# Dilated attention mix of a two-layer encoder: group weights turned once on TensorE and spread over the channels by DMAs from a DRAM scratch row, in place of copies and transposes

## The chip, the core and the metric

The kernel runs on one core of a Trainium2 chip. The metric is the device time of one execution in microseconds (us); lower is better.

## The reference, cut to what matters

A residual trunk of two layers (`DEPTH = 2`), 1024 tokens of 1024 channels, everything in float32. In each layer h = RMSNorm(x) goes through one input projection; its parts feed four mixers (Fourier, convolution, attention, pooling), each gated, projected by `w_branch[n]` and weighted by a sigmoid merge gate; the sum goes through `w_out`. The attention mixer runs three dilated window attentions of four heads each and mixes them by the softmax of their log-sum-exps, one weight for each token, head and group:

```
def dilated_mixture(qkv, cos, sin):
    ...
    for g, (window, dil) in enumerate(DILATED_CFG):            # 3 groups
        o, l = dilated_window_attention(q[:, :, g], k[:, :, g], v[:, :, g], dil, window // (2 * dil))
        ...
    alpha = jax.nn.softmax(jnp.stack(lses, axis=0), axis=0)
    out = outs[0] * alpha[0][..., None].astype(outs[0].dtype)
    for g in range(1, N_ATT_GROUPS):
        out = out + outs[g] * alpha[g][..., None].astype(outs[g].dtype)
```

The kernel computes the same weights from each group's maximum m and denominator d: alpha_g = exp(m_g - max m) / sum over the groups of d exp(m - max m), with the outputs of a group not yet divided.

## The kernel before

Activations lie channels by tokens: a tile is 128 channels x 512 tokens, tokens in two halves `hf`. Matrix products run with operands split in a high and a low part (three matmuls a product). The four heads are two head pairs `hp` (two heads x 64 channels = 128 partitions), so `att_mix` (L556) runs once for each head pair in each layer, four times in all. Names in this text: the **mix** is one run of `att_mix`; the first mix of a layer belongs to hp 0, the second to hp 1.

Order of the work. `layer` (L1135) writes one long stream of products; `att_group` and `att_mix` are generators in lanes. After every second pair of a main product, `passes` (L123) calls `tick`, which moves each lane one step, up to its next `yield`; `self.wait(n)` yields n times. So a mix's instructions are strewn between the matmuls that stand there. The first mix of a layer falls among the products of the second head pair's q, k, v; the second at the end of the input projection (tile z) and the start of the branch projections (tile py, `branch` L930, weights wr loaded at L116, split by ACT at L105 and DVE at L106). Each engine runs its own list in order, SP issues nearly all DMAs, and an instruction that waits holds up all behind it on its engine.

One mix before: maxima and sums on tiles of 128 tokens x 16 (8 token tiles x 2 heads), three exps of 128x16 on ACT (L572), weights es[g]. Then for each half and each group, six times: DVE copies a group's weights over the 64 channels of a head (tile fx, 128 tokens x 512, L588); SP loads the group's outputs, channels by tokens, from DRAM (tile og, L590); four PE transposes turn fx into a PSUM bank (tile fb, L594, one of the five `aux` banks); DVE multiplies og by fb (L595) and adds up (L597). The sum goes to DRAM (att, L600), one DMA for each half.

What stands around the second mix: `gate_evac` (L603) computes gates (ACT sg, L609; DVE gp, L610). `branch` runs over the four branches in the order pool, Fourier, attention, convolution. The inputs of a branch are made by `gated` (L906): for each of four quarter tiles, a load from a parked DRAM tensor (tile unpark, L926; `park` for pooling, `four`, `att`, `conv`), then a split into g, the high part on ACT (L105), the low part on DVE (L106). Branch outputs y leave PSUM by ACT (L938) and go to DRAM by SP (L939). fx, og, unpark, y, sg and others share one pool of twelve 128x512 tiles (`t2`, L94).

Of the kernel before, what the change touches and what calls it, by code (L numbers as in the profile page):

```python
# [9 lines left out]
F32 = mybir.dt.float32  # L10
F32R = mybir.dt.float32r
AF = mybir.ActivationFunctionType
ALU = mybir.AluOpType

P = 128
# [31 lines left out]
class Net:  # L47
# [505 lines left out]
        nc.sync.dma_start(out=nat, in_=sc.rearrange("(t p) c -> p t c", p=P))  # L553
        done.append((od, nat))

    def att_mix(self, groups, park):  # L556

        nc = self.nc
        while len(groups) < 3:
            yield  # L560
        yield from self.wait(4)
        sm = lambda nm: self.sm.tile([P, 8, 2], F32, tag="x" + nm, name="x" + nm, bufs=2)
        ms = [st[:, :, 0:2] for _, st in groups]
        ds = [st[:, :, 2:4] for _, st in groups]
        m = sm("m")
        nc.vector.tensor_tensor(out=m, in0=ms[0], in1=ms[1], op=ALU.max)
        nc.vector.tensor_tensor(out=m, in0=m, in1=ms[2], op=ALU.max)
        es = []
        for g in range(3):
            e = sm(f"e{g}")  # L570
            nc.vector.tensor_tensor(out=e, in0=ms[g], in1=m, op=ALU.subtract)
            nc.scalar.activation(out=e, in_=e, func=AF.Exp)  # L572
            es.append(e)
        z, t = sm("z"), sm("t")
        nc.vector.tensor_tensor(out=z, in0=ds[0], in1=es[0], op=ALU.mult)
        for g in (1, 2):
            nc.vector.tensor_tensor(out=t, in0=ds[g], in1=es[g], op=ALU.mult)
            nc.vector.tensor_tensor(out=z, in0=z, in1=t, op=ALU.add)
        nc.vector.reciprocal(out=z, in_=z)
        for g in range(3):  # L580
            nc.vector.tensor_tensor(out=es[g], in0=es[g], in1=z, op=ALU.mult)
        yield from self.wait(2)
        for hf in range(2):
            sl = slice(hf * H, hf * H + H)
            out = None
            for g in range(3):
                f = self.t2("fx").rearrange("p (t h c) -> p t h c", t=4, h=2)
                nc.vector.tensor_copy(out=f, in_=es[g][:, 4 * hf:4 * hf + 4].unsqueeze(3).to_broadcast([P, 4, 2, 64]))  # L588
                og = self.t2("og")
                nc.sync.dma_start(out=og, in_=groups[g][0][:, sl])  # L590
                yield from self.wait(4)
                ps = self.aux("fb")
                for j in range(4):
                    nc.tensor.transpose(ps[:, j * P:(j + 1) * P], f[:, j].rearrange("p h c -> p (h c)"), self.ident)  # L594
                nc.vector.tensor_tensor(out=og, in0=og, in1=ps, op=ALU.mult)  # L595
                if g:
                    nc.vector.tensor_tensor(out=out, in0=out, in1=og, op=ALU.add)  # L597
                else:
                    out = og
            nc.sync.dma_start(out=park[:, sl], in_=out)  # L600
# [534 lines left out]
    def layer(self, l):  # L1135
        nc = self.nc
        pool = self.pool(l)
        att = self.dr.tile([2, P, S], F32, name=f"att{l}")
        for hp in range(2):
            done = []  # L1140
            for g in range(3):
                self.att_group(l, hp, g, done)
            self.start("mix", self.att_mix(done, att[hp]))
        uf = [self.fourier_in(l, c) for c in range(2)]
        res, fy = [], []
        self.start("fou", self.fourier_pq(l, uf, res))
        self.start("fou", self.fourier_out(l, res, fy))
        conv = self.dr.tile([2, P, S], F32, name=f"conv{l}")
        gps = {0: [], 1: [], 2: []}
        four = self.dr.tile([2, P, S], F32, name=f"four{l}")  # L1150
        self.start("fou", self.gate_later(fy, gps[0], four))
        for hf in range(2):
            self.start("taps", self.conv_mix(l, hf, gps[1], conv))
        tf = {i: [] for i in range(1, 5)}
        g = {n: [] for n in range(4)}
        make = {0: self.gated(self.unpark(four), None, g[0]), 1: self.gated(self.unpark(conv), None, g[1]),
                2: self.gated(self.unpark(att), gps[2], g[2]), 3: self.gated(self.unpark(pool), None, g[3])}
        lanes = {0: ("fou",), 2: ("att", "mix"), 1: ("taps",), 3: ()}
        for n in GORDER:
            for c in range(2):  # L1160
                if (n, c) == (GORDER[2], 1):
                    self.start("g", make[YORDER[0]])
                gps[n].append(self.gate_path(l, n, c))
        for i, n in enumerate(YORDER):
            self.finish("g")
            if i < 3:
                for lane in lanes[YORDER[i + 1]]:
                    self.finish(lane)
                self.start("g", make[YORDER[i + 1]])
            if i == FORMS:  # L1170
                self.start("forms", self.token_forms(tf))
            self.branch(l, n, g[n])
        self.finish("forms")
        self.out_proj(l, self.gates(l, tf))
# [97 lines left out]
```

## Time and profile before

| | us |
|---|---|
| median of 3 runs | 1987.56 |
| lowest, highest | 1986.22, 1989.28 |
| profiled execution | 1990.16 |
| its span | 1988.4 |
| PE busy | 1948.0 (98%) |
| DVE busy | 1485.0 (75%) |
| ACT busy | 999.9 (50%) |
| DMA queue q1, share of 16 engines | 37.0% |

The span is the profiled part of the execution; 1.8 us lie outside it. PE is TensorE's matmuls, ACT is ScalarE, DVE is VectorE, SP the engine that issues DMAs. Times in rows are us from the span's start. The granted TensorE clock was 0.998 of full speed. Durations of successive matmuls overlap: what one costs on PE is the step from its start to the next start.

### The profile page before, as it was taken

To read this page: it belongs to the slowest core of one execution; us is meant where nothing else is said; L and a number is where in the kernel's file an instruction comes from. 1 tells how busy PE (TensorE), PEld (TensorE's weight loads), DVE (VectorE), ACT (ScalarE), POOL (GpSimd) and SP (SyncE) were. 2 spreads that over 40 slices of the span, in tenths; PEclk is the share of its full clock that TensorE was granted. 3 is DMA by queue.
4 is the path that set the end of the run, shared out by engine and by line. 5 is a ranking of instruction groups with operands and counts; after the bars stand their busy time and mean duration, and the time that the engine had idled before them with its cause. 6 is when DMAs were issued, how large, how long until landed. Compare 5 with 4: busy or idle time off the path is not lost.

```text
span 1988.4 us, 26782 instructions
## 1 busy us (share of the span) xinstructions
PE 1948.0 (98%) x9484; PEld 1624.7 (82%) x9484; DVE 1485.0 (75%) x2740; ACT 999.9 (50%) x1917; POOL 41.1 (2%) x90
## 2 busy tenths in 40 slices
PE   8999999999999999999999999999999999999997
PEld 6788887888888888887888888888888888888887
DVE  7598878886577777776655888888564877787764
ACT  6336655568574344444431456656775644443441
POOL 0000000000000000000000000000000000000000
PEclk9999999999999999999999999999999999999999
DMA  6243344423774433427421534433248823424443
GB/s 237 78 149 117 102 131 120 128 67 107 247 276 167 156 106 108 157 76 259 163 81 45 159 117 126 133 106 106 87 139 295 287 85 127 136 99 146 170 148 107
DMA packets 129446, 281.08 MB, mean 141 GB/s; under 512 B 32928, under 2 KB 37920, under 8 KB 129312
## 3 DMA queue, kind: packets, MB, share of 16 engines
q1 hardware_dynamic: 118368, 239.52, 37.0%
q0 software_dynamic: 10944, 39.85, 6.0%
q8 instruction: 75, 1.23, 0.3%
q14 instruction: 59, 0.48, 0.1%
HBM read 186.84 MB, written 67.30 MB: 128 GB/s over the span
## 4 chain that ended last, share of the span: by engine, by line
PE 81%; DVE 9%; ACT 4%; DMA 4%; issue 2%; SPq 0%; DVEq 0%; ACTq 0%
PE z L129 24%; PE ga L129 13%; PE g L129 9%; PE gb L129 8%; PE op L129 8%; PE py L129 8%; PE z L256 3%; DVE cv L849 2%; PE pv L129 2%; PE s L466 2%; PE pt L492 1%; DVE w L106 1%; ACT w L105 1%; ACT o L523 1%; DMA mt<-m 1%
## 5 line engine op out<-in xcount | busy, mean ns | idle before, releaser
L129 PE MATMUL z<-h,w 128*128 128x512 f32 x3000 | 741.4, 396 | 2.5 <-DVE gp L610 1.4
L129 PEld LDWEIGHTS z<-h,w 128*128 128x128 f32 x3000 | 546.8, 188 | 109.1 <-DVE gp L610 1.8
L106 DVE TENSOR_TENSOR w<-wr,w 128x1024 fp32r<-128x1024 f32 (+1 forms) x135 | 158.7, 1178 | 106.8 <-ACT w L105 90.9
L105 ACT ACTIVATE w<-wr 128x1024 fp32r<-128x1024 f32 (+1 forms) x135 | 137.9, 1023 | 172.7 <-PE z L129 80.3
L129 PE MATMUL g<-h,wf 128*128 128x512 f32 x768 | 184.5, 389 | 0.0
L129 PE MATMUL ga<-t,wf 128*128 128x512 f32 x768 | 184.5, 389 | 0.0
L129 PE MATMUL gb<-t,wf 128*128 128x512 f32 x768 | 184.5, 389 | 0.0
L129 PE MATMUL op<-m,w 128*128 128x512 f32 (+1 forms) x960 | 179.8, 348 | 2.8 <-DVE m L106 2.7
L849 DVE SCALAR_TENSOR_TENSOR cv<-cv,params 128x512 f32<-128x512 f32 x240 | 179.1, 746 | 2.3
L129 PE MATMUL py<-g,w 128*128 128x512 f32 x768 | 178.4, 391 | 0.8 <-DVE gp L610 0.5
L129 PEld LDWEIGHTS op<-m,w 128*128 128x128 f32 x960 | 153.9, 189 | 27.1 <-DVE m L106 4.4
L129 PEld LDWEIGHTS py<-g,w 128*128 128x128 f32 x768 | 143.1, 188 | 31.7 <-ACT y L938 1.3
L129 PEld LDWEIGHTS ga<-t,wf 128*128 128x128 f32 x768 | 144.2, 188 | 29.9
L129 PEld LDWEIGHTS gb<-t,wf 128*128 128x128 f32 x768 | 144.2, 188 | 29.9
L129 PEld LDWEIGHTS g<-h,wf 128*128 128x128 f32 x768 | 144.2, 188 | 29.9
L105 ACT ACTIVATE wf<-wr 128x512 fp32r<-128x512 f32 x144 | 91.0, 632 | 117.6 <-issue 46.3
L106 DVE TENSOR_TENSOR wf<-wr,wf 128x512 fp32r<-128x512 f32 x144 | 98.8, 686 | 19.4 <-ACT wf L105 18.1
L480 ACT ACTIVATE p<-p,nm 128x256 f32<-128x256 f32 (+2 forms) x192 | 87.9, 459 | 42.7 <-DVE nm L477 42.4
L105 ACT ACTIVATE wf<-s 128x512 fp32r<-128x512 f32 x64 | 40.5, 632 | 105.2 <-PE gb L129 62.6
L129 PE MATMUL ga<-h,wf 128*128 128x512 f32 x384 | 92.2, 389 | 0.0
L523 ACT ACTIVATE o<-pv 64x128 f32<-64x128 f32 x192 | 67.5, 351 | 48.1 <-PE pv L129 46.2
L129 PEld LDWEIGHTS ga<-h,wf 128*128 128x128 f32 x384 | 72.1, 188 | 15.0
(244 smaller groups left out, 2683.0 us busy)
## 6 DMA issues: line engine op xcount, KB each, us to landing
wr<-in_w_in_dram SPq DMA_DIRECT2D x75, 512.0 KB, 3.8
y<-y SPq DMA_DIRECT2D x128, 256.0 KB, 4.1
y<-y POOLq DMA_DIRECT2D x64, 512.0 KB, 4.8
wr<-in_w_gate_dram SPq DMA_DIRECT2D x48, 512.0 KB, 4.4
wr<-in_w_out_dram SPq DMA_DIRECT2D x32, 512.0 KB, 3.6
rot<-rt SPq DMA_DIRECT2D x192, 64.0 KB, 2.0
cv<-in_w_gate_dram SPq DMA_DIRECT2D x16, 512.0 KB, 4.9
wr<-in_w_branch_dram SPq DMA_DIRECT2D x16, 512.0 KB, 4.7
```

The source lines that it names most:

```text
L105: self.nc.scalar.activation(out=hi, in_=src, func=AF.Copy)
L106: self.nc.vector.tensor_tensor(out=lo, in0=src, in1=hi.bitcast(F32), op=ALU.subtract)
L129: self.nc.tensor.matmul(ps, w, x, start=(first and i + u == 0), stop=(i == n - 1 and u == 2), skip_group_check=open_)
L256: self.nc.tensor.matmul(ps, a[:, k], b, start=(k + j == 0), stop=(k == KC - 1 and j == 2))
L466: mm(s[i][h], q[h + j][:, qs], k[h][:, a:a + n], start=(j == 0), stop=(j == 2))
L480: nc.scalar.activation(out=ph, in_=ph, func=AF.Exp, bias=nm[:, h:h + 1], accum_out=st[:, t, 2 + h:3 + h])
L492: nc.tensor.transpose(pt[:rows[ci], cs], p[:, off:off + rows[ci]], self.ident)
L523: nc.scalar.activation(out=dst, in_=src, func=AF.Copy)
L849: self.tc.keep_in_program_order(nc.vector.scalar_tensor_tensor(out=y, in0=u[:, j:j + H], scalar=tap(j), in1=y, op0=ALU.mult, op1=ALU.add))
```

## The change

The three weight tiles are slices of one tile (xe, 128 x 48), so that one exp does for all groups. One PE transpose of 128 x 48 (tile et, an `aux` bank) puts (group, token tile, head) on 48 partitions and tokens in the free dimension; ACT copies it to SBUF (er), SP writes it to a DRAM tensor ed (24 KB). For each half and group two DMAs fill fx with channels on partitions: each reads four rows of 128 tokens of ed and writes them into 64 partitions (a source dimension of stride 0; 128 KB written in pieces of 512 bytes). DVE multiplies og by fx from SBUF. The copies (L588) and the fb transposes (L594) are gone, and the wait between og's load and its use is 3 steps instead of 4. `name` makes the DRAM tensor's name. All later line numbers grow by four.

```diff
@@ -553,7 +553,7 @@
         nc.sync.dma_start(out=nat, in_=sc.rearrange("(t p) c -> p t c", p=P))
         done.append((od, nat))
 
-    def att_mix(self, groups, park):
+    def att_mix(self, groups, park, name):
 
         nc = self.nc
         while len(groups) < 3:
@@ -565,12 +565,11 @@
         m = sm("m")
         nc.vector.tensor_tensor(out=m, in0=ms[0], in1=ms[1], op=ALU.max)
         nc.vector.tensor_tensor(out=m, in0=m, in1=ms[2], op=ALU.max)
-        es = []
+        ea = self.sm.tile([P, 3, 8, 2], F32, tag="xe", name="xe", bufs=2)
+        es = [ea[:, g] for g in range(3)]
         for g in range(3):
-            e = sm(f"e{g}")
-            nc.vector.tensor_tensor(out=e, in0=ms[g], in1=m, op=ALU.subtract)
-            nc.scalar.activation(out=e, in_=e, func=AF.Exp)
-            es.append(e)
+            nc.vector.tensor_tensor(out=es[g], in0=ms[g], in1=m, op=ALU.subtract)
+        nc.scalar.activation(out=ea, in_=ea, func=AF.Exp)
         z, t = sm("z"), sm("t")
         nc.vector.tensor_tensor(out=z, in0=ds[0], in1=es[0], op=ALU.mult)
         for g in (1, 2):
@@ -580,19 +579,24 @@
         for g in range(3):
             nc.vector.tensor_tensor(out=es[g], in0=es[g], in1=z, op=ALU.mult)
         yield from self.wait(2)
+
+        ps = self.aux("et")
+        nc.tensor.transpose(ps[:48, 0:P], ea.rearrange("p g t h -> p (g t h)"), self.ident)
+        er = self.t2("er")
+        nc.scalar.activation(out=er[:48, 0:P], in_=ps[:48, 0:P], func=AF.Copy)
+        ed = self.dr.tile([3, 8, 2, P], F32, name=f"ed_{name}")
+        nc.sync.dma_start(out=ed.rearrange("g t h p -> (g t h) p"), in_=er[:48, 0:P])
         for hf in range(2):
             sl = slice(hf * H, hf * H + H)
             out = None
             for g in range(3):
-                f = self.t2("fx").rearrange("p (t h c) -> p t h c", t=4, h=2)
-                nc.vector.tensor_copy(out=f, in_=es[g][:, 4 * hf:4 * hf + 4].unsqueeze(3).to_broadcast([P, 4, 2, 64]))
-                og = self.t2("og")
+                f, og = self.t2("fx"), self.t2("og")
+                for h in range(2):
+                    nc.sync.dma_start(out=f[64 * h:64 * h + 64].rearrange("p (t n) -> p t n", n=P),
+                                      in_=ed[g, 4 * hf:4 * hf + 4, h].unsqueeze(0).to_broadcast([64, 4, P]))
                 nc.sync.dma_start(out=og, in_=groups[g][0][:, sl])
-                yield from self.wait(4)
-                ps = self.aux("fb")
-                for j in range(4):
-                    nc.tensor.transpose(ps[:, j * P:(j + 1) * P], f[:, j].rearrange("p h c -> p (h c)"), self.ident)
-                nc.vector.tensor_tensor(out=og, in0=og, in1=ps, op=ALU.mult)
+                yield from self.wait(3)
+                nc.vector.tensor_tensor(out=og, in0=og, in1=f, op=ALU.mult)
                 if g:
                     nc.vector.tensor_tensor(out=out, in0=out, in1=og, op=ALU.add)
                 else:
@@ -1140,7 +1144,7 @@
             done = []
             for g in range(3):
                 self.att_group(l, hp, g, done)
-            self.start("mix", self.att_mix(done, att[hp]))
+            self.start("mix", self.att_mix(done, att[hp], f"{l}_{hp}"))
         uf = [self.fourier_in(l, c) for c in range(2)]
         res, fy = [], []
         self.start("fou", self.fourier_pq(l, uf, res))
```

Counts over the four mixes, from the loops: 24 DVE copies, 96 fb transposes in 24 groups of four, and 8 of 12 exps go; 4 et transposes, 4 er copies, 4 DMAs to ed and 48 DMAs ed to fx come (48 x 128 KB = 6.3 MB).

How the engines' lists change at three places. First SP's list in the first layer where the second mix begins, at the end of the input projection, before the change (`wr` of `w_branch` are branch weights, `park` is the parked pooling, `od` a group's outputs):

```order
L116 DMA wr<-in_w_branch_dram 128x1024
L590 DMA og<-od_1_0_3598 128x512
L926 DMA unpark<-park_84 128x512 x4
L116 DMA wr<-in_w_branch_dram 128x1024
L903 DMA conv_4044<-cz 128x512 x2
L590 DMA og<-od_1_1_4159 128x512
L590 DMA og<-od_1_2_4882 128x512
L926 DMA unpark<-four_4045 128x512
L939 DMA y_76<-y 128x512
```

and now:

```order
L116 DMA wr<-in_w_branch_dram 128x1024
L588 DMA ed_1_4964<-er 48x128
L595 DMA fx<-ed_1_4964 64x4x128 x2
L597 DMA og<-od_1_0_3584 128x512
L930 DMA unpark<-park_84 128x512 x3
L595 DMA fx<-ed_1_4964 64x4x128 x2
L597 DMA og<-od_1_1_4137 128x512
L930 DMA unpark<-park_84 128x512
L116 DMA wr<-in_w_branch_dram 128x1024
L907 DMA conv_4022<-cz 128x512 x2
L595 DMA fx<-ed_1_4964 64x4x128 x2
L597 DMA og<-od_1_2_4860 128x512
```

The four loads of unpark for the pooling branch stood behind one og load. Three now stand behind the DMA to ed, two fx DMAs that read ed, and an og; the fourth behind two more fx DMAs and another og.

Second, ACT's list at the same place, before (`csh` is the convolution's, `sg` a gate, `w` branch weights, `g` the pooling branch's input):

```order
L105 ACTIVATE csh<-cy 128x512
L609 ACTIVATE sg<-z 128x512
L105 ACTIVATE w<-wr 128x1024
L609 ACTIVATE sg<-z 128x512
L105 ACTIVATE g<-unpark 128x512 x4
L105 ACTIVATE w<-wr 128x1024
L609 ACTIVATE sg<-z 128x512
L938 ACTIVATE y<-py 128x512 x2
```

and now:

```order
L105 ACTIVATE csh<-cy 128x512
L613 ACTIVATE sg<-z 128x512
L586 ACTIVATE er<-et 48x128
L105 ACTIVATE w<-wr 128x1024 x2
L105 ACTIVATE g<-unpark 128x512 x3
L613 ACTIVATE sg<-z 128x512
L105 ACTIVATE g<-unpark 128x512
L613 ACTIVATE sg<-z 128x512
L942 ACTIVATE y<-py 128x512
```

er stands behind the first sg, and the second split of branch weights (w), which stood behind the four g, now stands before them.

Third, ACT's list at the same place in the second layer, now; before, four g stood ahead of the w:

```order
L613 ACTIVATE sg<-z 128x512
L586 ACTIVATE er<-et 48x128
L105 ACTIVATE g<-unpark 128x512 x3
L105 ACTIVATE w<-wr 128x1024
L613 ACTIVATE sg<-z 128x512 x2
L105 ACTIVATE g<-unpark 128x512
L942 ACTIVATE y<-py 128x512
```

er is ahead of three of the g, and the fourth is behind a w and two sg.

## Rows read from the trace of the kernel before

**Rows 1.** The page: its head, the busy time by engine (us, share of the span, instructions) and the first line of the chain that ended last (share of the span by engine).
```profile
span 1988.4 us, 26782 instructions
...
PE 1948.0 (98%) x9484; PEld 1624.7 (82%) x9484; DVE 1485.0 (75%) x2740; ACT 999.9 (50%) x1917; POOL 41.1 (2%) x90
...
PE 81%; DVE 9%; ACT 4%; DMA 4%; issue 2%; SPq 0%; DVEq 0%; ACTq 0%
```

**Rows 2.** Busy time by stretch of the span (columns: stretch, its length, then busy us of PE, of its weight loads, DVE, ACT and POOL with their instructions, the granted clock, the DMA share and GB/s). The first and the third hold the attention of the two layers, the second most of the first layer's branch projections, the last two their start.
```profile
180.00:420.00 240.00, 232.56 (x1244) 195.66 (x1245) 200.87 (x458) 137.14 (x349) 0.00 (x0) 1.00 0.40 115
520.00:604.00 84.00, 83.75 (x376) 68.50 (x375) 53.85 (x83) 53.66 (x95) 2.25 (x4) 1.00 0.85 293
1170.00:1470.00 300.00, 296.82 (x1624) 251.39 (x1623) 233.46 (x564) 195.69 (x460) 0.00 (x0) 1.00 0.37 109
500.00:520.00 20.00, 19.47 (x90) 15.77 (x89) 14.55 (x22) 10.65 (x17) 0.00 (x0) 1.00 0.60 208
520.00:540.00 20.00, 20.00 (x98) 16.48 (x97) 8.72 (x14) 12.28 (x21) 0.00 (x0) 1.00 0.92 302
540.00:560.00 20.00, 20.00 (x90) 16.45 (x89) 8.34 (x12) 10.76 (x21) 0.00 (x0) 1.00 0.82 277
```

**Rows 3.** What writes and reads the tile fb (engine, operation, count: ns min/median/max, first and last start).
```profile
L594 PE MATMUL fb<-consts,fx x96: 270/272/329, 322.3 to 1512.4; 128*128 128x128 f32 x96
```

**Rows 4.** What writes the tile fx.
```profile
L588 DVE COPY fx<-xe x24: 408/418/428, 317.4 to 1504.7; 128x512 f32<-128x512 f32 x24
```

**Rows 5.** What line 572 issues (the exps of the mix).
```profile
L572 ACT ACTIVATE xe<-xe x12: 199/208/219, 300.5 to 1462.3; 128x16 f32<-128x16 f32 x12
L572 ACT ACT_TABLE_LOAD  x4: 1283/1283/1283, 481.6 to 1461.0; - x4
```

**Rows 6.** Timeline of PE (start, length, engine, line, operation, tiles, shapes, count, and in brackets the idle time before it and what ended it) around one group of transposes in the first layer's attention.
```profile
322.26 0.60 PE L594 MATMUL fb<-consts,fx 128*128 128x128 f32 x4
322.62 1.17 PE L129 MATMUL z<-h,w 128*128 128x512 f32 x4
```

**Rows 7.** The same, around two places in the attention where PE stood still.
```profile
342.15 0.66 PE L594 MATMUL fb<-consts,fx 128*128 128x128 f32 x4 [1.07 <-ACT o L523]
...
355.90 0.60 PE L594 MATMUL fb<-consts,fx 128*128 128x128 f32 x4
357.61 1.66 PE L129 MATMUL z<-h,w 128*128 128x512 f32 x6 [1.10 <-ACT rt L371]
```

**Rows 8.** The same, in the second layer's attention.
```profile
1318.95 0.66 PE L594 MATMUL fb<-consts,fx 128*128 128x128 f32 x4 [1.08 <-ACT o L523]
```

**Rows 9.** PE at the change from the input projection to the first branch projection, first layer.
```profile
508.53 0.60 PE L594 MATMUL fb<-consts,fx 128*128 128x128 f32 x4
...
513.11 1.52 PE L129 MATMUL py<-g,w 128*128 128x512 f32 x6
```

**Rows 10.** SP's DMA issues there.
```profile
501.97 0.42 SPq L590 DMA_DIRECT2D og<-od  x1
502.49 3.00 SPq L926 DMA_DIRECT2D unpark<-park  x4
```

**Rows 11.** ACT there.
```profile
505.68 0.58 ACT L609 ACTIVATE sg<-z 128x512 f32<-128x512 f32 x1
508.50 1.06 ACT L105 ACTIVATE w<-wr 128x1024 fp32r<-128x1024 f32 x1 [2.24 <-PE cp L129]
...
509.94 2.18 ACT L105 ACTIVATE g<-unpark 128x512 fp32r<-128x512 f32 x4
513.09 1.07 ACT L105 ACTIVATE w<-wr 128x1024 fp32r<-128x1024 f32 x1 [0.96 <-PE z L129]
```

**Rows 12.** DVE a little later, in the same mix.
```profile
523.66 0.42 DVE L588 COPY fx<-xe 128x512 f32<-128x512 f32 x1
523.99 0.68 DVE L106 TENSOR_TENSOR g<-unpark,g 128x512 fp32r<-128x512 f32 x1
```

**Rows 13.** Issues of DMAs over the whole run (destination and source, queue, count, KB each, median us from issue to landing).
```profile
sc<-st SPq DMA_DIRECT2D x16, 4.0 KB, 1.6
...
nat<-sc SPq DMA_DIRECT2D x8, 16.0 KB, 2.3
sc<-st SPq DMA_DIRECT2D x8, 8.0 KB, 3.7
```

**Rows 14.** DMAs that write or read the tile sc (DRAM, where an attention group's statistics are turned through): least, median and longest time from issue to landing, us.
```profile
DMA to landing us min/median/max: 1.5/2.5/6.0
```

**Rows 15.** DMAs that fill the tile unpark: least, median and longest time from issue to landing, us.
```profile
DMA to landing us min/median/max: 2.5/4.5/6.5
```

**Rows 16.** DMAs that fill the tile og or store it: least, median and longest time from issue to landing, us.
```profile
DMA to landing us min/median/max: 2.0/3.9/7.1
```

**Rows 17.** The same change from projection to branch in the second layer: SP's issues.
```profile
1477.10 2.02 SPq L926 DMA_DIRECT2D unpark<-park  x4
```

**Rows 18.** The same in the second layer: ACT.
```profile
1477.89 0.58 ACT L609 ACTIVATE sg<-z 128x512 f32<-128x512 f32 x1
...
1488.30 1.06 ACT L105 ACTIVATE w<-wr 128x1024 fp32r<-128x1024 f32 x1 [3.56 <-PE z L129]
```

**Rows 19.** The same in the second layer: PE.
```profile
1488.33 1.53 PE L129 MATMUL py<-g,w 128*128 128x512 f32 x6
```

## The prediction

> **What bounds the kernel now.** I read the busy times and the chain first [rows 1]: PE is busy 98% of the span and makes 81% of the chain, DVE 9%. So an edit counts by what it takes from or adds to PE's list, and by waits that it puts into that list or takes out; time of DVE, ACT and SP counts only where PE ends up waiting for it. Then the stretches [rows 2]: in the attention of the two layers PE is idle 240 - 232.56 = 7.4 us and 300 - 296.82 = 3.2 us; from 520 on, in the branch projections, hardly at all, while the DMA engines are at 0.85 (0.92 from 520 to 540). The granted clock is 1.00 in every stretch, the upper of its two levels, so it plays no part in the sum. The mix runs in both surroundings: the first of a layer in the attention, the second where the branch projections begin. I take these apart.
>
> **The transposes that go.** The 96 fb transposes last 272 ns each [rows 3], but they overlap. A group of four starts at 322.26 and the product behind it at 322.62 [rows 6]: 0.36 us a group, 24 x 0.36 = 8.6 us. The Trainium skill (TensorE: Matmul & The Clock Gate, Part 4: PE-mode transpose) gives about 275 ns for one in a kernel; as a duration the trace agrees (272 ns), as a price it differs, 0.36 us for four, and the trace decides; by the page's figure as a price 26 us would go.
>
> One of the 24 groups stands right ahead of a product that waited 1.10 us for ACT's rt [rows 7]: PE would come there earlier and wait longer, so 0.4 us are given back.
>
> **Waits that go with them.** Two fb groups waited 1.07 and 1.08 us for ACT's o [rows 7, 8]: they wanted a PSUM bank that ACT had not emptied. Without the group the next work is a product into another bank, so I take all 2.1 us; the bounds are 0 (the wait falls on the next user of such a bank) and 2.1.
>
> **What PE gets instead.** Four et transposes of 128 x 48. Nearest: 0.09 us as a part of a group, 0.36 for a whole one [rows 6]. I take 0.12 each, 0.5 in all, bounds 0.4 and 1.4.
>
> **DVE and ACT.** The 24 copies (418 ns [rows 4], step 0.33, from 523.66 to 523.99 [rows 12]) free 24 x 0.33 = 7.9 us of DVE; 8 of 12 exps free 0.2 us each, and part of 4 table loads of 1.28 us [rows 5]. ACT gets 4 er copies, about 0.3 us each (estimate: a 128 x 16 exp takes 0.21 [rows 5]). PE's waits that could profit are the idle time above; in the sum I take none, and keep it as a rival. The multiply reads SBUF instead of PSUM, at the same size; I cost that at nothing, since DVE's waits hide it.
>
> **SP and the DMAs, first mixes.** 52 DMAs more, at 0.42 us an issue [rows 10] 22 us of SP in four stretches. In the first mix of each layer the order puts weights and rotary loads behind them, but each by a couple of us, in a stretch where the engines' share is 0.40 and 0.37 [rows 2]; fx is issued beside og, so the multiply waits for og or for fx at about the same time. I take 0, bounds 0 and 2 us for both layers.
>
> **The second mix of the first layer.** Here the order decides. SP held the four unpark loads at 502.49 [rows 10]; the four g were ready by 509.94 + 2.18 = 512.12 on ACT [rows 11], and py began without a wait at 513.11 [rows 9]. Now they stand behind ed and fx. er follows the sg that ends at 505.68 + 0.58 = 506.26 [rows 11], so 506.6. ed lands 1.6, 3.7 or 2.3 us after its issue by the small transfers through DRAM [rows 13]; it is nearest to the 16 KB one, so 2.3: 508.9. Two fx and one og at 0.42: 510.2. An unpark lands in 4.5 us [rows 15]: 514.7. The split of one g takes 0.55 (2.18 for four [rows 11]): 515.2, its low part on DVE about 0.6 more. PE, one fb group earlier [rows 9], wants it at 513.11 - 0.36 = 512.75. That makes 2.5 us for the first matmul and 3.0 with the low part. The fourth quarter, behind two more fx and an og, is ready at about 517.8 (low part 518.4) where the product wants it at 517.8: 0.5 more. **+3.5 us.** The least is not 0 even with fast DMAs: on ACT a split of weights now stands ahead of the g, and it waited for the last z and took 1.07 [rows 11]; from 512.75 it ends at 513.8, g at 514.4: about 2.0. The most, with ed at 6.0 [rows 14] and unpark at 6.5 [rows 15], is about 9.3.
>
> The rest of that mix lies under the branch projection. att, which SP now has ahead of three loads for the next branch, waits for the third multiply; its tile og lands within 7.1 us [rows 16], and the next branch starts some 20 us after the first (a quarter of the 84 us [rows 2]), so this is covered; if it were not, the next branch's first product would stand, in the same way.
>
> **The second mix of the second layer.** sg ends at 1477.89 + 0.58 [rows 18], er at 1478.8, ed at 1481.1, the first unpark at 1482.4 (it was 1477.10 [rows 17]), landed at 1486.9, g at 1487.4; PE wants it at 1488.33 - 0.36 = 1487.97 [rows 19]: in time. The fourth g now stands behind a w that waits for PE's last z [rows 18] and behind two sg: 1488.0 + 1.06 + 2 x 0.58 + 0.55 = 1490.8, low part 1491.4, wanted at about 1490.0. **+1.1 us**, bounds 0.8 and 6.5.
>
> **Sum.** -8.6 + 0.4 - 2.1 + 0.5 + 3.5 + 1.1 = -5.2 us. The profiled execution took 1990.16 us (span 1988.4 [rows 1] and 1.8 around it) and would take 1985.0; it is 2.6 us above the median, so for a median I take 1987.56 - 5.2 = **1982.4**. Of this the 24 groups are sure; the tails are the soft part. With the bounds of the terms the forecast itself runs from 1979.5 to 1986.
>
> **Rivals.** Measured differences under 0.2% (4.0 us) can't be told from none; so faster means under 1983.6, slower over 1991.5.
>
> *Relief of DVE and ACT.* 7.9 us of DVE go, and PE is idle 10.6 us in the two attentions [rows 2], of which 3.3 are counted above. If half of the other 7.3 goes, another -3.7: 1978.7. For it: DVE is 84% busy in that stretch of the first layer (200.87 of 240). Against it: the waits that I looked at there end with ACT [rows 7, 8].
>
> *Nothing left.* The steps saved in the first mixes (12 x 0.36 less 0.4) and the 2.1 us of waits, 6.0 us, fall to other waits of a stretch that has them: 1988.4. For it: the product behind the group at 355.90 shows just that [rows 7].
>
> *Slower: the way through DRAM at the start of the branches.* The unpark loads are bound to ed's landing, since SP issues in order. With landings at the longest shown, the two tails are 9.3 + 6.5 = 15.8 us instead of 4.6: 1982.4 + 11.2 = 1993.6. It decides from a sum of the two tails of 13.8 us on (the other terms give -9.8). For it: no row shows a read of one DRAM row by 64 partitions, and unparks would share the queue with it. Against: medians are far below.
>
> *DMA engines full.* 12 fx DMAs a mix carry 1.57 MB. At the rate of 520 to 540 (302 GB/s at 0.92 [rows 2], so 328 at full) they take 4.8 us; free are 0.40 x 20 + 0.08 x 20 = 9.6 us between 500 and 540. If each held the engines for the 1.6 us in which the smallest transfer lands [rows 13], it would be 19.2, 9.6 too many; if half of that reaches PE through late y writes, 2 x 4.8 us: 1992.0. The Trainium skill (DMA: Bandwidth & Descriptors, Bandwidth) gives 138 GB/s for a transfer of 64 KB and 341 for one of 1 MB; by the lower rate a mix's fx would take an estimated 11.4 us, 1.8 more than is free. No row here shows such a transfer.
>
> *Transposes at their full length.* If a group cost 4 x 272 ns [rows 3], 26.1 us would go instead of 8.6: 1964.9. Starts in the timeline [rows 6] speak against it.
>
> **Chances and range.** Forecast 0.44, relief 0.12, nothing left 0.20, slow way through DRAM 0.14, DMA engines full 0.06, full length 0.04. About two thirds of the forecast's own range lie under 1983.6: 0.29 + 0.12 + 0.04 = 0.45 faster; the rest of it, nothing left, and the mild ends of the two slow cases, 0.15 + 0.19 + 0.03 = 0.37 the same; 0.18 slower. The range from 1976 to 1994 takes in the tails' upper bounds and the relief, and leaves out the full length and the ends of the others.
>
> **What would show it.** Right: no fb on PE, four et; no wait of a py product before 510 but one of 2 to 4 us at about 513, ended by ACT's or DVE's g, and one of about 1 us near 1490; ed landing in 2 to 3 us. Wrong: py starting without a wait (the tails are nothing), a wait of 8 us there (the DRAM way), a DMA share of 1 from 505 to 540 with y waiting, or waits in the attention that grow by what was saved.

## The result: 1998.1 us, slower by 0.5%

The changed kernel takes 1998.14 us (median of 4 runs, 1996.31 to 2000.17), the kernel before 1988.42 (4 runs, 1986.22 to 1989.29): a ratio of 1.0051, 95% interval 1.0038 to 1.0063. 1982.4 was forecast, so even the sign was wrong, and 1998.1 is above the upper end of the range. The profiled execution took 1999.93 us, with a span of 1998.0 where it was 1988.4 [rows 1].

The page of the change, busy times by engine:

```profile
PE 1948.1 (98%) x9392; PEld 1619.2 (81%) x9392; DVE 1477.7 (74%) x2716; ACT 993.7 (50%) x1910; POOL 41.1 (2%) x90
```

PE is as busy as before (1948.1 us), without 96 transposes, and waits are not counted as busy: the matmuls that are left take longer, and PE waits besides. What the products of the branch projections (py) waited for most over the whole span, in the change and then before (total us, times, longest):

```profile
PE py L129 <- ACT y L942: 12.2, 8, 3.8
```

```profile
PE py L129 <- ACT y L938: 0.2, 1, 0.2
```

In the change py also waited 1.7 us for ACT's g and 1.3 us for DVE's g. The timeline of PE in the first layer, from the first py product on:

```profile
508.01 0.50 PE L129 MATMUL py<-g,w 128*128 128x512 f32 x1 [1.71 <-ACT g L105]
509.08 18.36 PE L129 MATMUL py<-g,w 128*128 128x512 f32 x71 [0.57 <-DVE g L106]
529.06 17.98 PE L129 MATMUL py<-g,w 128*128 128x512 f32 x78 [1.63 <-ACT y L942]
549.27 1.91 PE L129 MATMUL py<-g,w 128*128 128x512 f32 x6 [2.23 <-ACT y L942]
551.79 2.93 PE L129 MATMUL py<-g,w 128*128 128x512 f32 x6 [0.61 <-ACT y L942]
555.76 53.17 PE L129 MATMUL py<-g,w 128*128 128x512 f32 x222 [1.04 <-ACT y L942]
```

and the first product behind the branch projections, in the change and then in the kernel before:

```profile
608.77 1.07 PE L129 MATMUL g<-h,wf 128*128 128x512 f32 x4
```

```profile
604.35 0.84 PE L129 MATMUL g<-h,wf 128*128 128x512 f32 x3
```

py began at 513.11 before [rows 9] and at 508.01 now: PE came to the branch projections 5.1 us sooner. It left them at 608.77 instead of 604.35, 4.4 us later: 9.5 us were lost on the way, though five fb groups (1.8 us) are gone from it. In the second layer the same (first py product, then two of the later waits, then the first product behind the branch projections, in the change and before):

```profile
1489.06 0.50 PE L129 MATMUL py<-g,w 128*128 128x512 f32 x1
...
1529.96 1.65 PE L129 MATMUL py<-g,w 128*128 128x512 f32 x6 [1.06 <-ACT y L942]
1535.43 53.14 PE L129 MATMUL py<-g,w 128*128 128x512 f32 x222 [3.82 <-ACT y L942]
```

```profile
1588.41 1.30 PE L129 MATMUL g<-h,wf 128*128 128x512 f32 x5
```

```profile
1577.85 0.84 PE L129 MATMUL g<-h,wf 128*128 128x512 f32 x3
```

From 1488.33 [rows 19] to 1577.85 it was 89.5 us, now 99.4: 9.9 us lost. The two branch stages cost 19.4 us; all else gained 9.8 (the first layer 5.1 up to py, of which 1.9 lie ahead of the first place that the change touches; then, with PE 4.4 us late behind the first layer's stage and 0.7 at the second layer's, 3.7; the last stretch 0.9 or so). The difference of the spans, 9.6, is that.

The lost time has two parts. In the first layer PE waits inside the stage for 0.57 + 1.63 + 2.23 + 0.61 + 1.04 = 6.1 us (7.4 in the second layer). The rest of 9.5 + 1.8, 5.2 us, is not waits; the granted clock accounts for about that much. Stretches of the change (columns as in [rows 2]), and one of before:

```profile
500.00:560.00 60.00, 52.16 (x200) 40.18 (x199) 26.27 (x36) 25.53 (x44) 0.00 (x0) 0.89 0.77 259
510.00:520.00 10.00, 10.00 (x39) 8.08 (x39) 6.46 (x11) 2.77 (x6) 0.00 (x0) 0.85 0.80 261
540.00:550.00 10.00, 7.77 (x35) 6.13 (x34) 3.83 (x5) 3.12 (x4) 0.00 (x0) 1.00 0.79 271
550.00:560.00 10.00, 8.34 (x21) 5.59 (x20) 4.05 (x6) 4.70 (x10) 0.00 (x0) 0.53 0.72 257
1530.00:1540.00 10.00, 6.18 (x17) 4.61 (x18) 2.82 (x5) 5.24 (x10) 0.00 (x0) 0.68 0.71 270
```

```profile
500.00:560.00 60.00, 59.47 (x274) 48.70 (x273) 31.61 (x47) 33.68 (x58) 0.00 (x0) 1.00 0.78 262
```

Behind the waits around 550 the granted clock has a mean of 0.53 for 10 us: nearly all of it at the lower of the two levels, 1.2 GHz. A shorter stretch at that level lies behind the waits at the start of the stage (0.85 from 510 to 520). Six py products take 2.93 us at 551.79, and 1.65 at 1529.96, which is at the upper level. And over this stretch the DMA engines are no busier than before: 0.77 and 259 GB/s from 500 to 560, against 0.78 and 262.

**Where y comes from.** y is the copy by which ACT empties a PSUM bank of py. A product that waits for y waits for a free bank. ACT's list at that time:

```profile
537.56 0.60 ACT L942 ACTIVATE y<-py 128x512 f32<-128x512 f32 x1 [0.60 <-PE py L129]
545.95 0.63 ACT L105 ACTIVATE g<-gt 128x512 fp32r<-128x512 f32 x1 [7.79 <-DVE gt L921]
546.48 2.25 ACT L105 ACTIVATE w<-wr 128x1024 fp32r<-128x1024 f32 x2
548.64 0.58 ACT L942 ACTIVATE y<-py 128x512 f32<-128x512 f32 x1
```

ACT empties a bank at 537.56, and then stands 7.79 us before g of the attention branch, with the y of the finished banks queued behind it. That g waits for DVE's gt, and gt for the load unpark<-att:

```profile
535.78 0.69 DVE L599 TENSOR_TENSOR og<-og,fx 128x512 f32<-128x512 f32 x1 [3.69 <-DMA og<-od]
...
545.22 0.69 DVE L921 TENSOR_TENSOR gt<-unpark,gp 128x512 f32<-128x512 f32 x1 [8.03 <-DMA unpark<-att]
...
547.56 2.43 DVE L106 TENSOR_TENSOR w<-wr,w 128x1024 fp32r<-128x1024 f32 x2 [0.26 <-ACT w L105]
```

And SP's list there, in the change, and then the same loads before:

```profile
537.22 0.32 SPq L604 DMA_DIRECT2D att<-og  x1
537.63 2.37 SPq L943 DMA_DIRECT2D y<-y  x5
540.06 0.56 SPq L930 DMA_DIRECT2D unpark<-att  x1
540.67 1.12 SPq L116 DMA_DIRECT2D wr<-in_w_branch_dram  x2
...
542.38 0.43 SPq L930 DMA_DIRECT2D unpark<-att  x1
548.81 0.33 SPq L116 DMA_DIRECT2D wr<-in_w_branch_dram  x1
549.19 0.43 SPq L930 DMA_DIRECT2D unpark<-att  x1
```

```profile
537.53 1.11 SPq L926 DMA_DIRECT2D unpark<-att  x1
...
541.88 0.32 SPq L600 DMA_DIRECT2D att<-og  x1
...
542.73 1.36 SPq L926 DMA_DIRECT2D unpark<-att  x2
```

Before, the first unpark<-att left SP 4.4 us ahead of att's second store (it reads what the first mix stored, long ago). Now it stands behind that store, which waits for the mix's last multiply (535.78; its og left SP at 531.80, behind the group's two fx), and behind five y: 540.06. The third load stands behind a load of branch weights, which waits for a buffer that DVE's w frees at 547.56 and later, whose ACT part stands behind the first g. So it leaves at 549.19 where it left by 544 before, though PE came to these branches sooner than before: a chain from a load over DVE, ACT, DVE and SP to the next load.

### The profile page after: what moved, and what is told of

Read it like the earlier page. It is cut to its first block, busy times and chain, and to the rows that moved or that the text cites. A ratio compares the mean times of both kernels' runs of the same rounds, so it can differ in the third digit from the quotient of the medians.

```text
span 1998.0 us, 26633 instructions
## 1 busy us (share of the span) xinstructions
PE 1948.1 (98%) x9392; PEld 1619.2 (81%) x9392; DVE 1477.7 (74%) x2716; ACT 993.7 (50%) x1910; POOL 41.1 (2%) x90
## 4 chain that ended last, share of the span: by engine, by line
PE 75%; DVE 11%; DMA 7%; ACT 4%; issue 2%; SPq 1%; DVEq 0%; ACTq 0%
PE z L129 23%; PE ga L129 13%; PE g L129 9%; PE gb L129 8%; PE op L129 6%; PE py L129 6%; DVE cv L853 3%; PE pv L129 2%; PE z L256 2%; DVE w L106 2%; PE s L466 2%; PE pt L492 1%; ACT w L105 1%; DMA mt<-m 1%; DMA wr<-in_w_out_dram 1%
## 5 line engine op out<-in xcount | busy, mean ns | idle before, releaser
L129 PE MATMUL py<-g,w 128*128 128x512 f32 x768 | 186.9, 404 | 15.3 <-ACT y L942 12.2
L129 PEld LDWEIGHTS py<-g,w 128*128 128x128 f32 x768 | 148.1, 195 | 54.1 <-ACT y L942 17.5
```

Source lines behind the costliest of these rows:

```text
L129: self.nc.tensor.matmul(ps, w, x, start=(first and i + u == 0), stop=(i == n - 1 and u == 2), skip_group_check=open_)
```

## The experiments

Theory A: the loss belongs to the second mix of a layer, by the order of SP's list at the third branch. The third branch is the attention mixer's. Rivals: B, PE's gains are eaten by the branch stage whatever makes them; the DMA engines' load; the pieces of 512 bytes. Ratios are to the kernel before, run on the same chip, with 95% intervals.

**One mix alone.** `att_mix_old` is the function of before, added to the class:

```diff
-            self.start("mix", self.att_mix(done, att[hp], f"{l}_{hp}"))
+            mix = self.att_mix(done, att[hp], f"{l}_{hp}") if hp == 0 else self.att_mix_old(done, att[hp])
+            self.start("mix", mix)
```

> The new mix for head pair 0 alone, the old one for head pair 1. The new trace lost its time in the second mixes: PE's lag against before went from -6.9 to +5.1 us in the first layer's branch projections and from +1.5 to +10.6 in the second's, while the two attentions gained 3.5 and 2.4 us. Theory A (the loss belongs to the second mix's own loads and waits): both gains stay, 1988.4 - 6 = 1982, and the py products wait for ACT's y less than 1 us in all. Theory B (the branch stage cannot start its third branch before att's loads, whatever PE gained before): the gains are eaten there, 1987 to 1989.

Measured 1980.65 us, ratio 0.996 (0.9947 to 0.9973), 7.0 us faster; py no longer waits for y at all. With `hp == 1` in place of `hp == 0`:

> The old mix for head pair 0, the new one for head pair 1. Theory A: the whole loss of the branch stages without the gains of the attentions, 1998.1 + 6 = 2004. Theory B: the second mix sets an end of its own, so what PE gains or loses before does not matter, about 1998 again.

Measured 2005.71, ratio 1.0094 (1.0077 to 1.0111), 18 us slower; py waits 14.0 us for y. The gains of the first mixes are real and stay, the second mixes lose 18 us, and the sum, +11, agrees with the change's own +10. B falls.

**Who issues, and nothing issued.**

```diff
-        nc.sync.dma_start(out=ed.rearrange(...
+        nc.gpsimd.dma_start(out=ed.rearrange(...
-                    nc.sync.dma_start(out=f[64 * h:64 * h + 64]...
+                    nc.gpsimd.dma_start(out=f[64 * h:64 * h + 64]...
```

> The whole change, with the DMA to ed and the fx DMAs issued by POOL instead of SP; bytes and pieces are the same. If SP's order makes the loss (unpark, og and y behind DMAs that wait for ed or for each other), py's wait for ACT's y falls from 12.2 us to below 4 and the time to 1985 to 1990. If it is the DMA engines' load, it stays at 1996 to 2000.

Measured 1993.91, ratio 1.0028 (1.0017 to 1.004): between the two. y's part fell from 12.2 to 4.8 us, not quite below the 4 that SP's order would have, and another wait came:

```profile
PE py L129 <- DVE g L106: 8.2, 2, 5.2
```

DVE stood 3.80 us for fx ahead of the multiply, with g's low part behind it:

```profile
509.85 0.69 DVE L599 TENSOR_TENSOR og<-og,fx 128x512 f32<-128x512 f32 x1 [3.80 <-DMA fx<-ed]
510.46 0.68 DVE L106 TENSOR_TENSOR g<-unpark,g 128x512 fp32r<-128x512 f32 x1
```

The wait was moved from SP's list to DVE's. And without any fx DMA:

```diff
-                for h in range(2):
-                    nc.sync.dma_start(out=f[64 * h:64 * h + 64]...
+                nc.gpsimd.memset(f, 1.0)
```

> The 48 fx DMAs are left out: fx is a constant 1 written by POOL, so the weights are not applied (ed is still written). No fx bytes and no fx issues. If the DMA load makes the loss, 1982 to 1985 and clearly below the kernel that issues them by POOL; if SP's order does, the same as that one within 3 us.

Measured 1974.05, ratio 0.9933 (0.9918 to 0.9948). That is what the change would give if fx cost nothing: between no fx DMA and all of them lie 24 us. By the expectation it would speak for the load, as it is 20 us below the kernel that issues by POOL. But it is also far below the 1982 to 1985 named for the load, and it takes away bytes, issues and the wait for fx at once, so it does not tell load from order. SP's list near att's second store in this run:

```profile
524.69 0.32 SPq L602 DMA_DIRECT2D att<-og  x1
...
529.52 0.43 SPq L928 DMA_DIRECT2D unpark<-att  x1
```

The loads stand behind the store here too, and py waits for y only 2.6 us in all. So it is not the fx DMAs in SP's list that put the loads behind the store; which part of the edit did, no run takes alone. And that order costs little as long as the store comes early.

**Order alone.** `unpark` with its load given an early place (`high_priority` asks for an instruction to be listed earlier where its data allow it), nothing added or taken away:

```diff
-            self.nc.sync.dma_start(out=t, in_=park[c, :, sl])
+            with self.tc.high_priority(offset=AHEAD):
+                self.nc.sync.dma_start(out=t, in_=park[c, :, sl])
```

> The whole change, with the loads of the branch inputs (unpark) put on SP's list as early as their data allows: the attention branch's first one ahead of att's second store, and the third ahead of the next load of branch weights. Nothing is added or taken away. Order theory (the loss at the third branch comes from where these loads stand on SP and, through ACT's list, from y behind g): the waits of py for ACT's y go from 12.2 us to below 5 and about 6 to 10 us come back, 1988 to 1992. If the loss is the traffic or the latency of fx itself, at most 2 us come back.

> The same edit on the kernel before, as the other side of the comparison: there py waits for ACT's y only 0.2 us, so nothing to win; within 2 us of before, whichever theory holds.

Measured 1981.2 us with the change, ratio 0.9964 (0.9953 to 0.9975), and 1990.72 on the kernel before, 1.0013 (1.0004 to 1.0022), 2.9 us slower, a little outside what was expected. So the same edit is worth 17 us to the change, more than the 6 to 10 expected, and nothing to the kernel before. SP's list in the change with it:

```profile
535.70 0.32 SPq L931 DMA_DIRECT2D unpark<-att  x1
536.42 0.32 SPq L604 DMA_DIRECT2D att<-og  x1
536.79 0.93 SPq L944 DMA_DIRECT2D y<-y  x2
537.81 0.41 SPq L931 DMA_DIRECT2D unpark<-att  x1
538.28 2.29 SPq L944 DMA_DIRECT2D y<-y  x3
540.66 0.55 SPq L931 DMA_DIRECT2D unpark<-att  x1
...
542.38 0.45 SPq L116 DMA_DIRECT2D wr<-in_w_branch_dram  x1
```

The first unpark<-att leaves ahead of att's second store, the third ahead of the weights, at 540.66 instead of 549.19, with the same fx DMAs. py's wait for y:

```profile
PE py L129 <- ACT y L943: 4.9, 4, 2.3
```

Only the attention branch's loads early (`self.unpark(att, AHEAD)`, the others as they were):

> The whole change, with the early place on SP's list for the attention branch's four loads alone (the first ahead of att's second store and its five y, the third ahead of the next branch weights); all else as in the change. Putting all branches' loads early gave 1981.2 against 1998.1. If the third branch's loads are the loss, this alone gives nearly all of it, 1981 to 1985; if the Fourier branch's loads had a share, it stays above 1988.

Measured 1984.17, ratio 0.9984 (0.9975 to 0.9994), with 4.7 us of waits for y: 13 to 14 of the 17 us come back with the place of these four loads in each layer. In both runs the lists of ACT and DVE moved along: in the first layer the two splits of branch weights (w), which stood right behind the first g in the change, now stand behind the third g and later. So the place is settled, the order around the third branch's loads; the share of each instruction in it is not.

**Size of pieces, number of DMAs.** ed as (group, head, token tile, token), with xe laid out the same way ahead of the transpose:

```diff
...
-        ed = self.dr.tile([3, 8, 2, P], F32, name=f"ed_{name}")
+        ed = self.dr.tile([3, 2, 8, P], F32, name=f"ed_{name}")
...
-                                      in_=ed[g, 4 * hf:4 * hf + 4, h].unsqueeze(0).to_broadcast([64, 4, P]))
+                                      in_=ed[g, h, 4 * hf:4 * hf + 4].rearrange("t p -> (t p)").unsqueeze(0).to_broadcast([64, H]))
```

> The whole change with ed laid out (group, head, token tile, token), so that each fx DMA reads one run of 2 KB for each partition instead of four of 512 bytes: same bytes, same DMAs, a quarter of the pieces, and SP's, ACT's and PE's lists in the same order. If small pieces make the loss (slow DMAs, slow issues), fx lands 1 us or more sooner and 4 us or more come back; if order and the number of DMAs do, it stays within 2 us of 1998.

Measured 1995.77, ratio 1.0039 (1.0028 to 1.005), 2.4 us under the change's median, with an interval that overlaps the change's own; fx landed in 3.9 us instead of 4.0, and py waited 12.6 us for y. The pieces are not the cause.

```diff
+                nc.gpsimd.memset(f[64:128], 1.0)
-                for h in range(2):
+                for h in range(1):
```

> Half of the fx DMAs (24 instead of 48): the second head's half of fx is a constant 1 written by POOL, so its weights are not applied. Without any fx DMA the time was 1974.1, with all 1998.1. If it is a dose of DMAs (issue time on SP or traffic), about the middle, 1984 to 1988. If it is the chain ed, fx, multiply and the order that comes of it, nearly as slow as all, 1994 to 1998, since each group still waits for one.

Measured 1983.94, ratio 0.9981 (0.9971 to 0.9991): the dose counts. SP's list still has the attention loads in the change's order, yet att's second store left at 531.91 instead of 537.22, and y's part was 7.1 us. So two things make the loss together: fx DMAs that hold att's store back, and loads that stand behind it. Removing half of the first, or all of the second, each gives about 14 us or more. Counted from the first py product of the first layer, the store leaves 18.8 us on without fx DMAs, 25.2 with half of them, 29.2 with all, and 28.8 in the kernel before: it is hardly later than it was, but now the loads are behind it. Whether the issues or the bytes of fx hold it back is not separated.

**The start of the branches, and the rest.** With all branch inputs early, the pooling branch's loads and splits one projection unit sooner:

```diff
-                if (n, c) == (GORDER[2], 1):
+                if (n, c) == (GORDER[2], 0):
                     self.start("g", make[YORDER[0]])
```

> As the version with all branch inputs loaded early (1981.2), and the pooling branch's four loads and splits started one projection unit sooner, so that SP issues them ahead of ed instead of behind ed and fx, and ACT splits them ahead of er. If the wait at the start of the branch projections (2.3 us and its low clock in the first layer, about 1 us in the second) comes from their place behind ed and fx, it goes: 1976 to 1979, and py starts without a wait. If py then waits for something else there, 1981.

> The same two edits on the kernel before: there py starts without a wait and the third branch hardly waits, so they have nothing to win; within 3 us of before.

Measured 1978.6, ratio 0.9958 (0.9943 to 0.9973), not clear of the 0.9964 without the second edit, and 1988.11 on the kernel before, 1.0003 (0.9993 to 1.0013). py begins without a wait:

```profile
508.00 7.19 PE L129 MATMUL py<-g,w 128*128 128x512 f32 x31
```

and its waits for ACT's y are 3.8 us in all. This is the whole change with two edits of order, and it beats both kernels; the first mix alone (1980.65) is as good within the intervals. Some 5 us still lie between it and the run without fx DMAs (1974.05), which no run takes apart.

> The whole change with ed and fx issued by POOL (1993.9 alone) and all branch inputs early (1981.2 alone). If what is left of SP's issue time of 48 fx DMAs still costs, 1976 to 1979. If POOL's slower way (fx landed 0.6 to 2 us later, and DVE's multiply held up g behind it for 3.0 and 5.2 us) costs more than it saves, 1981 to 1988.

Measured 1987.8, ratio 1.0 (0.999 to 1.0009): y's part is gone (0.8 us), but DVE's g holds py 6.5 us. With the order right, POOL's way costs more than SP's issue time. The Trainium skill (DMA: Bandwidth & Descriptors, Rules for kernel authors) says that spreading DMAs over issuing engines does not help bandwidth and only saves issue time. The runs agree: in the two layers' branch stages fx landed in 4.5 and 6.7 us (median) in the first run that issued by POOL and 4.8 and 5.3 here, against 3.9 and 4.5 from SP.

## Why the prediction was wrong

- *The transposes (-8.6) and the waits with them (-2.1)* held as far as the first mixes show. There the terms give 12 x 0.36 + 2.1 - 0.4 and 0.2 for et, -5.8; the first mix alone measured -7.0, with an interval that holds it. The run gives the sum, not each term.
- *et, er, ed, fx singly* were small or as taken; first ed, from issue to landing, then fx, its issue on SP (ns) and its landing:

```profile
DMA to landing us min/median/max: 1.4/1.4/1.4
```

```profile
L595 SPq DMA_DIRECT2D fx<-ed x48: 573/615/1271, 316.5 to 1509.2; - x48
...
DMA to landing us min/median/max: 2.8/4.0/6.0
```

  For ed 2.3 us were taken and 1.4 measured; fx lands about as og does (3.4 median in the change). The read of one DRAM row by 64 partitions, which no row had shown, is not slow. An fx issue takes 0.6 us of SP instead of the 0.42 taken.
- *The tails at the start of the branches (+3.5 and +1.1)* are there, smaller: PE waited 1.71 + 0.57 us in the first layer (with the low clock from 510 to 520 behind it, which no term held), 0.2 to 0.3 three times in the second. SP's part, as foretold, ed to unpark:

```profile
499.84 0.32 SPq L588 DMA_DIRECT2D ed<-er  x1
501.31 1.30 SPq L595 DMA_DIRECT2D fx<-ed  x2
...
503.36 1.32 SPq L930 DMA_DIRECT2D unpark<-park  x3
```

  ed left SP at 499.84, fx 1.5 us later, unpark at 503.36. With the pooling branch's loads ahead of ed the wait in front of the first py is gone, though the 2.6 us between the two medians are not clear of noise. So most signs that were named for being right came true (no fb, four et, the wait at the first py), in a kernel that was slower: none of these looked at the third branch.
- **The step that failed** is "The rest of that mix lies under the branch projection ... so this is covered", a cost put at 0. It looks at att's first store, behind the third multiply, and at the second branch; there PE did wait, 1.63 us in the first layer and 0.62 in the second. For att's second store and the third branch the sum has no term. At that end of SP's list the first load of the attention branch stood behind the second store, and the third behind weights that wait for that branch's own g. The cover for y, the PSUM banks, ended there: y waited on ACT behind g, and products of the branch that was running stood: 2.23 + 0.61 + 1.04 us in the first layer and 1.20 + 1.06 + 3.82 in the second, 10.0 of the 12.2 us of py's waits for y. The step had named a wait ("if it were not, the next branch's first product would stand"), but for the wrong product and without a price. The early place of these four loads alone gave 13 to 14 us back.
- *The clock* was said to play no part in the sum, and that failed too. Of the time lost in the two stages (19.4 us and twice the 1.8 of the fb groups), 13.5 are waits; most of the other 9.5 are products at the lower level behind the waits (0.53 from 550 to 560, 0.68 from 1530 to 1540).
- *The range of the forecast itself* does not follow from its terms: with the stated bounds they add up to 1980.5 to 1998.6, not to 1979.5 to 1986. That 1998.1 lies inside is luck, since those upper bounds belong to the tails, which came out smaller.
- *The rival on the slow side* had the right list and the wrong place: SP's order, but at the start of the branches. *DMA engines full* is refuted: from 500 to 560 their share did not rise, and an edit that left every byte in place gave 17 us back. *Nothing left* is refuted: gains made in the first mixes stay. *Relief of DVE and ACT* can't be told from the first mix's 7.0 us.

## What to carry to other kernels

Where a change alters an in-order queue of DMAs, read the whole new order of that queue up to the last consumer of the result, not only the place where the first of them stands: what costs is a load that someone needs soon, behind a store that is late. Price the end of a lane like its start, and count that an engine which waits behind such a load (here ACT, with the copies that free PSUM banks queued behind it) stops others. Before giving up an edit that lost, move only the order: here two edits of order turned +0.5% into -0.4%.

## What the runs showed of the hardware

Reading the same 512-byte rows of DRAM into 64 partitions took about as long as an ordinary load of twice the size (fx 4.0 us median; og 3.9 before [rows 16] and 3.4 in the change), and pieces four times as large changed that by 0.1 us. Short waits can cost nearly as much again: behind waits of 2.23 and 0.61 us the granted clock was 0.53 for 10 us, and of the 11.3 us lost in that stage (9.5 and the 1.8 of the fb groups) 5.2 are not waits. Not every wait does it: behind the 1.63 us at 529.06 the clock stayed at 1.00 until 550. With the new mix in the first place alone, where py has no wait for y, it is 1.00 in every 10 us from 490 to 570.
